# Modulation rows copied into weight order, one normalizing operation in place, and an earlier first gather

## The chip, the core and the metric

The kernel runs on one core of a Trainium2 chip. Its time is the device time of one execution, in microseconds (us). A core has five engines that run their own instruction queues in order: TensorE (PE, matrix products; its weight loads are listed as PEld), VectorE (DVE), ScalarE (ACT), GpSimd (POOL) and SyncE (SP, which only issues DMAs). POOL and ACT issue DMAs too.

## The reference, cut to what matters

Two layers work on 256 latent tokens and 256 context tokens of width 1024. Each layer has a mixer (attention, with an output projection) and then a mixture of 16 experts, two of which are chosen per token. Between them stands the part that the change touches:

```
x = x + g1 * y                                   # y: the mixer after its output projection
h = rms_norm(x) * (1 + sc2) + sh2                # rows sc2, sh2 differ for latent and context tokens
x = x + g2 * hierarchical_moe(h, ...)            # top-1 group, top-2 experts of 16
```

Layer 0 does this for latent and context tokens (four blocks of 128 tokens), layer 1 for the latent ones only (two blocks).

## The kernel before, in words

**Tiles.** `xt` holds the token blocks (tb) as 128 tokens by 1024 columns. `out_project` (L482) multiplies the mixer's result with the output weights in two halves of 512 columns (h) and, in each half, block by block (n). Every product is three matmuls of rounded parts (`mm3`, L315); the parts are made by `split` (L311), a cast on ACT and a subtraction on DVE. At the end of a block DVE scales the product by the row g1 (L497) and adds it to `xt` (L499), and `x_ready` (L1082) is called; `hook` (L1125) is called after each of the eight steps kt and places small work between the matmuls: folding the modulation into the router weights (`fold_mod`), transposes of `xt` (`x_turned`), router logits (`logits`).

**Normalization.** `x_ready` sums squares on ACT (L1086). After the second half it makes 1/rms (L1088, L411, L412) and the normalized block `h2[tb]` in two operations: L1092 multiplies `xt` by 1/rms and by the scale row, L1094 adds the shift row. The expert weights are stored with columns in another order ("weight order": column q*8+k goes to place k*128+q), so `h2` is written in that order, and L1092 and L1094 read `xt` and the rows with a step of 8 numbers (`by_part`, L1021). L1094 runs on DVE, but for the last block on POOL:

```
V.scalar_tensor_tensor(xp, by_part(xt[:, tb, :], KT), ss[:, tb, 4:5], scale, op0=ALU.mult,
                       op1=ALU.mult)
(G if tb == tbs[-1] else V).tensor_tensor(out=xp, in0=xp, in1=shift, op=ALU.add)
```

In layer 0 POOL then writes `h2` to DRAM (L1096). The rows are broadcast to all partitions by DMAs that POOL issues (`mod_row`, L372). One tile `rows` with one buffer holds both rows of a token kind, so that the context rows are fetched when the latent rows have been read. In layer 0 `h2` has a tile of its own; in layer 1 it stands in `xt[:, 2:4]`, which attention has used before.

**Experts.** After the last logits come some matmuls that only keep PE busy (`warm`, L226) and the routing on DVE (L1168 to L1453). The experts' work is cut into blocks of 128 slots, each with a gate (G), an up (U) and a down (D) product. Block 0 takes its tokens from `h2` by one-hot matmuls (`pick`, L1274). In layer 0 the later blocks fetch theirs from DRAM: `fetch_rows` (L1226) makes eight one-hot matrices on DVE (L1357), multiplies them on PE (L1233), sums to an index (L1237), and POOL issues a gather (L1239); `x_turn` (L1396) transposes the rows (L1409). `fetch_to` (L1414) is called in `gate_up` (L1623) after a gate product and asks for the rows of up to five blocks ahead. Expert weights are loaded by SP in pieces of 2 MB (L211) into a ring of buffers, each load waiting for a buffer to come free; most depend on the routing, which names the expert.

**Order.** A planner places the instructions of each engine by priority (the order of the program text) and by its own estimates of when they are ready; each engine then runs its list in order.

Of the kernel before, what the change touches and what calls it, by code (L numbers as in the profile page):

```python
# [11 lines left out]
F32 = mybir.dt.float32  # L12
# [4 lines left out]
ALU = mybir.AluOpType  # L17
AX = mybir.AxisListType

P = 128  # L20
D = 1024
KT = 8
# [143 lines left out]
def hybrid_kernel(ctx: ExitStack, tc: tile.TileContext, A: dict, dbg=None):  # L166
    nc = tc.nc
    V, S, T, G = nc.vector, nc.scalar, nc.tensor, nc.gpsimd
# [25 lines left out]
    def right(name):  # L194
        return Open(name, "right")
# [21 lines left out]
    def mm(name="mm"):  # L217
        return psum.tile([P, 512], F32, name=name, tag="mm", bufs=5)
# [15 lines left out]
    xt = pool.tile([P, 4, D], F32, name="xt")  # L234
# [42 lines left out]
    def load_router(wk, l):  # L277
        w = wk.tile([P, KT, 32], F32, name="wrt")
        V.memset(w, 0.0)
        G.dma_start(w[:, :, 0:4], A["w_group"][l].rearrange("(k p) g -> p k g", p=P))  # L280
        G.dma_start(w[:, :, 4:20], A["w_router"][l].rearrange("(k p) g -> p k g", p=P))
        return w
# [16 lines left out]
    h2d = dram.tile([512, D], F32, name="h2d")  # L299
# [72 lines left out]
    def mod_row(dst, l, seg, v, queue=G):  # L372

        queue.dma_start(dst, modd[l][seg, v:v + 1, :].to_broadcast([P, D]))
# [35 lines left out]
    def rstd_of(dst, ss, n, tmp):  # L410
        S.activation(tmp, ss, AF.Sqrt, bias=eps, scale=1.0 / n)  # L411
        V.reciprocal(dst, tmp)  # L412
# [608 lines left out]
    def by_part(a, k):  # L1021

        return a.rearrange("p (q k) -> p k q", k=k)

    def parted(a, k):

        return a.rearrange("p (k q) -> p k q", k=k)
# [5 lines left out]
    def moe(l, ntb, experts, yp, yT, finish, w_o, place, after_loads):  # L1033
        NT = 128 * ntb
        nv = (ntb + 1) // 2
        caps = CAPS[l]
        tbs = tuple(range(ntb))
# [7 lines left out]
        h2 = [xt[:, 2 + tb, :] if l else rows_of[:, tb, :] for tb in tbs]  # L1045
# [4 lines left out]
            experts.issue(1)  # L1050
        wk = right("out")
        wrt = load_router(wk, l)
        g1, rows = [], []
        for v in range(nv):
            g1.append(wk.tile([P, D], F32, name="g1", bufs=nv))
            mod_row(g1[v], l, 2, v)
        for v in range(nv):
            rows.append(wk.tile([P, 2, D], F32, name="rows", bufs=1))
            mod_row(rows[v][:, 0, :], l, 4, v)
            mod_row(rows[v][:, 1, :], l, 3, v)  # L1060

        wm = [wk.tile([P, KT, 32], F32, name="wm", bufs=1) for v in range(nv - 1)] + [wrt]
        crow = [wk.tile([P, 20], F32, name="crow", bufs=nv) for v in range(nv)]
# [1 line left out]
        def fold_mod(v):  # L1065
            sh, sc = (modr[l][:, i, :, v:v + 1].to_broadcast([P, KT, 32]) for i in range(2))
            t = wk.tile([P, KT, 32], F32, name="wsh", tag="rs", bufs=2)
            V.tensor_tensor(out=t, in0=wrt, in1=sh, op=ALU.mult)
            part = wk.tile([P, 32], F32, name="part", bufs=nv)
            V.reduce_sum(part, t.rearrange("p k e -> p e k"), axis=AX.X)  # L1070
            V.tensor_tensor(out=wm[v], in0=wrt, in1=sc, op=ALU.mult)
            if v == 0:
                V.memset(full, 1.0)
            ps = mm("crow")
            T.matmul(ps[:, 0:32], full, part, start=True, stop=True)
            V.tensor_tensor(out=crow[v], in0=ps[:, 0:20], in1=bias[:, 20 * l:20 * l + 20], op=ALU.add)

        full = wk.tile([P, P], F32, name="full", tag="lT", bufs=1)
        ss = wk.tile([P, ntb, 5], F32, name="ss")
        xT, pr, written = {}, [], []  # L1080

        def x_ready(h, tb):  # L1082

            c = slice(512 * h, 512 * h + 512)
            sq = wk.tile([P, 512], F32, name="sq", tag="rs", bufs=2)
            S.activation(sq, xt[:, tb, c], AF.Square, accum_out=ss[:, tb, h:h + 1])  # L1086
            if h:
                V.tensor_tensor(out=ss[:, tb, 2:3], in0=ss[:, tb, 0:1], in1=ss[:, tb, 1:2], op=ALU.add)  # L1088
                rstd_of(ss[:, tb, 4:5], ss[:, tb, 2:3], D, ss[:, tb, 3:4])
                xn = h2[tb]  # L1090
                xp, scale, shift = parted(xn, KT), *(by_part(rows[tb // 2][:, i, :], KT) for i in range(2))
                V.scalar_tensor_tensor(xp, by_part(xt[:, tb, :], KT), ss[:, tb, 4:5], scale, op0=ALU.mult,  # L1092
                                       op1=ALU.mult)
                (G if tb == tbs[-1] else V).tensor_tensor(out=xp, in0=xp, in1=shift, op=ALU.add)  # L1094
                if l == 0:
                    written.append(G.dma_start(h2d[128 * tb:128 * tb + 128, :], xn))  # L1096

        def x_turned(h, tb):
            pt = tr()
            for j in range(4):  # L1100
                kt = 4 * h + j
                T.transpose(pt[:, 128 * j:128 * j + 128], xt[:, tb, 128 * kt:128 * kt + 128], ident)
            xT[h, tb] = wk.tile([P, 4, P], F32, name=f"xT{h}", bufs=2 - h)
            (S.copy if h else V.tensor_copy)(xT[h, tb], pt.rearrange("p (k t) -> p k t", k=4))
# [20 lines left out]
        def hook(h, n, kt):  # L1125
            if h == 0 and n == 0 and finish:
                next(steps, None)
            if h == 0 and n == 1 and kt in (3, 6) and kt < 3 * nv + 3:
                fold_mod(kt // 3 - 1)
            if h == 1 and kt == 2:  # L1130
                x_turned(0, tbs[n])
            if h == 1 and n and kt == 4:
                x_turned(1, tbs[n - 1])
            if h == 1 and n >= 1 and kt >= KT - 2:
                if kt == KT - 2:
                    lgs[n - 1] = logits(tbs[n - 1])
                next(lgs[n - 1])
# [88 lines left out]
        def fetch_rows(i, hot):  # L1226
# [9 lines left out]
            with nc.allow_low_precision("whole numbers below 512"):  # L1236
# [5 lines left out]
        fixed_of = [[(r - experts.known, n_) for _, n_, r in b] for b in blocks  # L1242
                    if min(r for _, _, r in b) >= experts.known]
# [79 lines left out]
        for nm in ("base", "cap"):  # L1323
            t = un.tile([P] + sq, F32, name="cmp_" + nm, tag="aT", bufs=AB)
# [27 lines left out]
        def fetch(i):  # L1352

            def hot(o, tb, k):
                c = 0
                for s0, n_ in runs(i):
                    V.tensor_scalar(o[:, c:c + n_], C("iota128")[:, 0:n_], float(s0), slot[k][:, tb:tb + 1],  # L1357
                                    op0=ALU.add, op1=ALU.is_equal)
                    c += n_

            fetch_rows(i, hot)
# [52 lines left out]
        def fetch_to(i):  # L1414
            while l == 0 and fetched[0] < min(i, len(blocks)):
                fetch(fetched[0])
                fetched[0] += 1
# [212 lines left out]
        def down(bi, amid, final):  # L1630
# [29 lines left out]
            else:  # L1660
# [8 lines left out]
                if bi == len(blocks) - 2:  # L1669
                    for _ in range(3):  # L1670
                        experts.issue(1, queue=S)

        for i, (which, bi) in enumerate(ops):
            now[0] = i
            before = ops[i - 1] if i else None
            then = ops[i + 1] if i + 1 < len(ops) else None
            final = l == 0 and bi == len(blocks) - 1

            def amid(k):
                if k == 1 and then and then[0] == 0:  # L1680
                    x_turn(then[1])
                if k == 3 and final and which == 0:
                    weigh_last()
                if k == 2 and before and before[0] == 1:
                    for q in range(2):
                        a_turn(before[1], q)

            if final and which == 0:
                inorder = tc.manual_schedule(engines={mybir.EngineType.DVE, mybir.EngineType.Activation,
                                                      mybir.EngineType.PE})  # L1690
                inorder.__enter__()
            if which < 2:
                gate_up(which, bi, amid)
            else:
                down(bi, amid if before != (1, bi) else lambda k: amid(k) if k != 2 else None, final)
            if final and which == 0:
                for tb, tag, bufs in ((2, "xg", 2), (3, "xTb", XB)):
                    done = gather(tb, [un.tile([P, D], F32, name="yg", tag=tag, bufs=bufs) for k in range(2)])
                    pass
                after_loads(gather(0, [g2[:, nv + k, :] for k in range(2)]))  # L1700
            if final and which == 2:
                inorder.__exit__(None, None, None)
            if l and i == 0:
                ready(0, hot_rows(0))
# [4 lines left out]
        with tc.If(rv > 0):  # L1709
# [17 lines left out]
            with tc.For_i(0, NE, 1) as e:  # L1727
# [3 lines left out]
                with tc.If(nc.values_load(some[0:1, 0:1], min_val=0, max_val=1) > 0):  # L1731
# [7 lines left out]
                    for tb in range(ntb):  # L1739
# [4 lines left out]
                        for half in range(2):  # L1744
                            pt = tr()
                            for j in range(4):
                                kt = 4 * half + j
# [21 lines left out]
                        for h in range(2):  # L1769
                            ps = tr("dn")  # L1770
                            for f in range(4):
                                T.matmul(ps, aT[:, f, :], ws[2][:, f, 512 * h:512 * h + 512], start=(f == 0), stop=(f == 3))
                            t = un.tile([P, DE], F32, name="sg", bufs=SG)
                            V.scalar_tensor_tensor(t, ps, rc[:, tb:tb + 1], g2[:, tb // 2, 512 * h:512 * h + 512],
                                                   op0=ALU.mult, op1=ALU.mult)
# [7 lines left out]
        if l:  # L1783
            for tb, h in itertools.product(tbs, range(2)):
                c = slice(512 * h, 512 * h + 512)
                xn = un.tile([P, 512], F32, name="xn", tag="aT" if h else "sg", bufs=2)
# [75 lines left out]

    w_o, w_out = w_out, []
    rest, close_moe, gathers, tail = moe(0, 4, ex, yp, yT, None, w_o, place, after0)

    loads1 = [lambda: load_out("w_out_odd")]
# [51 lines left out]
```

## Time and profile before

| | us |
|---|---|
| median of 3 runs | 1079.56 |
| lowest, highest | 1076.38, 1085.37 |
| profiled execution | 1080.66 |
| its span in the trace | 1078.9 |
| PE busy in the span | 986.9 |
| DVE, ACT, POOL busy | 562.4, 385.0, 54.3 |

The span runs from the first to the last instruction in the trace; 1.8 us of the profiled execution lie around it. Busy times are sums; whether an engine holds up the others is read from the idle time in front of the waiting instructions.

### The profile page before, as it was taken

How to read it: one execution, taken by the hardware profiler on the slowest of the kernel's cores; microseconds unless marked ns; L12 is line 12 of the kernel's file. 1: busy time of each engine (PE TensorE's matmuls, PEld its weight loads, DVE VectorE, ACT ScalarE, POOL GpSimd, SP SyncE). 2: the span in 40 equal slices, each digit the busy share in tenths (PEclk: the TensorE clock that was granted, in tenths of full speed). 3: DMA queues.
4: the chain of work that ended last, by engine and by line, in shares of the span. 5: the costliest groups of instructions: out<-in, count | busy, mean ns of one | idle time of the engine just before them, and what ended most of it. 6: DMA issues, size and time to landing. Idle time of an engine off the chain costs nothing. (4 is left out here: it accounts for less than half of the span.)

```text
span 1078.9 us, 14186 instructions
## 1 busy us (share of the span) xinstructions
PE 986.9 (91%) x5205; PEld 579.3 (54%) x5205; DVE 562.4 (52%) x1346; ACT 385.0 (36%) x811; POOL 54.3 (5%) x75
## 2 busy tenths in 40 slices
PE   4899999896979989999987999998897999999995
PEld 3666555684543636567422668885566444434532
DVE  3565465767553636369316745627878323214324
ACT  4254343432132515368214525326853310100111
POOL 3000100102000000000021000000011000000000
PEclk8899999997989989999999999999997999999998
DMA  9969877525777999888896684234064899969891
GB/s 287 364 244 388 335 316 278 197 92 191 278 318 286 389 425 429 341 345 344 337 366 233 250 334 140 98 145 164 20 228 174 364 426 427 426 285 418 359 404 40
DMA packets 52546, 309.81 MB, mean 287 GB/s; under 512 B 4432, under 2 KB 12832, under 8 KB 35064
## 3 DMA queue, kind: packets, MB, share of 16 engines
q1 hardware_dynamic: 42440, 277.01, 64.9%
q0 software_dynamic: 5984, 19.26, 5.0%
q10 hardware_dynamic: 4048, 12.59, 3.1%
q8 instruction: 43, 0.70, 0.3%
q14 instruction: 31, 0.25, 0.1%
HBM read 299.85 MB, written 8.98 MB: 286 GB/s over the span
## 5 line engine op out<-in xcount | busy, mean ns | idle before, releaser
L1649 PE MATMUL dn<-we,aT 128*64 128x512 f32 (+2 forms) x480 | 119.4, 605 | 2.8 <-DMA we<-in_w_down_dram 2.7
L1616 PE MATMUL gu<-we,xT 128*64 128x512 f32 (+1 forms) x512 | 113.7, 611 | 1.7 <-DMA we<-in_w_up_dram 1.7
L1616 PE MATMUL gu<-we,xt 128*32 128x512 f32 (+2 forms) x448 | 104.9, 596 | 0.0
L312 ACT CAST wh<-we 128x512 fp32r<-128x512 f32 x144 | 85.4, 620 | 51.9 <-PE dn L317 28.5
L316 PE MATMUL mm<-wh,hT 128*128 128x512 f32 x248 | 101.5, 409 | 1.8 <-ACT hT L312 1.8
L313 DVE TENSOR_TENSOR wl<-we,wh 128x512 fp32r<-128x512 f32 x144 | 92.8, 685 | 17.2 <-ACT wh L312 11.3
L317 PE MATMUL mm<-wh,hT 128*128 128x512 f32 x248 | 98.5, 397 | 0.4 <-DVE hT L313 0.4
L318 PE MATMUL mm<-wl,hT 128*128 128x512 f32 x248 | 98.4, 397 | 0.0
L1649 PEld LDWEIGHTS dn<-we,aT 128*64 128x64 f32 (+2 forms) x480 | 36.4, 134 | 68.0 <-issue 62.1
L1616 PEld LDWEIGHTS gu<-we,xt 128*32 128x32 f32 (+2 forms) x448 | 36.5, 136 | 58.1 <-issue 56.2
L1616 PEld LDWEIGHTS gu<-we,xT 128*64 128x64 f32 (+1 forms) x512 | 32.9, 133 | 59.9 <-issue 56.6
L313 DVE TENSOR_TENSOR wl<-wi,wh 128x512 fp32r<-128x512 f32 x52 | 35.6, 688 | 50.1 <-ACT wh L312 35.0
L1627 DVE TENSOR_TENSOR sg<-sg,gu 128x256 f32<-128x256 f32 x40 | 15.2, 416 | 85.2 <-PE gu L1616 83.4
L316 PEld LDWEIGHTS mm<-wh,hT 128*128 128x128 f32 x248 | 47.3, 191 | 19.1 <-issue 7.3
L312 ACT CAST wh<-wi 128x512 fp32r<-128x512 f32 x52 | 32.1, 621 | 67.1 <-PE mm L317 62.8
L317 PEld LDWEIGHTS mm<-wh,hT 128*128 128x128 f32 x248 | 47.2, 190 | 11.5 <-issue 1.7
L318 PEld LDWEIGHTS mm<-wl,hT 128*128 128x128 f32 x248 | 47.1, 190 | 11.4 <-issue 0.8
L1622 ACT ACTIVATE sg<-gu 128x512 f32<-128x512 f32 x20 | 11.9, 596 | 90.6 <-PE gu L1616 84.5
L312 ACT CAST y<-y 128x512 fp32r<-128x512 f32 x16 | 9.9, 618 | 94.1 <-DVE y L1547 81.2
L345 PE MATMUL ada<-wada,cs 128*32 128x512 f32 x320 | 41.2, 619 | 2.4 <-DMA wada<-in_w_ada_dram 2.4
L316 PE MATMUL mm<-wo,yT 128*128 128x512 f32 x96 | 39.6, 413 | 2.4 <-ACT wo L312 2.4
L1357 DVE TENSOR_SCALAR oh<-cst,slots 128x128 bf16<-128x128 f32 (+1 forms) x96 | 23.4, 280 | 34.4 <-PE tok L1233 33.5
(364 smaller groups left out, 1675.3 us busy)
## 6 DMA issues: line engine op xcount, KB each, us to landing
we<-in_w_gate_dram SPq DMA_DIRECT2D x32, 2048.0 KB, 22.8
we<-in_w_up_dram SPq DMA_DIRECT2D x31, 2048.0 KB, 17.8
we<-in_w_down_dram SPq DMA_DIRECT2D x30, 2048.0 KB, 19.3
wada<-in_w_ada_dram SPq DMA_DIRECT2D x24, 2048.0 KB, 12.0
wi<-in_w_in_odd_dram SPq DMA_DIRECT2D x6, 2048.0 KB, 7.9
win<-in_w_in_even_dram SPq DMA_DIRECT2D x2, 2048.0 KB
wo<-in_w_out_even_dram SPq DMA_DIRECT2D x2, 2048.0 KB, 8.4
we<-in_w_down_dram ACTq DMA_DIRECT2D x2, 2048.0 KB, 13.8
```

The source lines that it names most:

```text
L312: S.copy(hi, src)
L313: V.tensor_tensor(out=lo, in0=src, in1=hi.bitcast(F32), op=ALU.subtract)
L316: T.matmul(ps, a[0], b[0], start=start, stop=False)
L317: T.matmul(ps, a[1], b[0], start=False, stop=False)
L318: T.matmul(ps, a[0], b[1], start=False, stop=stop)
L345: T.matmul(ps[32 * j:32 * j + 32], cs[:, kt, :], w[:, k, 512 * j:512 * j + 512], start=(kt == 0), stop=(kt == KT - 1))
L1357: V.tensor_scalar(o[:, c:c + n_], C("iota128")[:, 0:n_], float(s0), slot[k][:, tb:tb + 1], op0=ALU.add, op1=ALU.is_equal)
L1616: T.matmul(ps[c:c + n_], xTs[bi][0][:, kt, c:c + n_], experts.w[r, which][:, kt, :], start=(kt == 0), stop=(kt == KT - 1))
L1622: S.activation(parted(sgs[bi], 4), by_part(ps, 4), AF.Silu)
L1627: V.tensor_tensor(out=sg[:, c], in0=sg[:, c], in1=up[:, c], op=ALU.mult)
L1649: T.matmul(ps[h][c:c + n_], aTs[bi][0][:, f, c:c + n_], experts.w[r, 2][:, f, 512 * h:512 * h + 512], start=(f == 0), stop=(f == 3))
```

## The change

The scale and shift rows are fetched by DMA into tiles of `h2` that are not in use yet, and ACT copies them into weight order into tiles of their own (`take_row`): two scale tiles in layer 0 and one in layer 1, and one shift tile. `x_ready` no longer multiplies by the scale row with 1/rms. Instead `scaled` multiplies `xt` by the scale row, one half of the columns at a time: the first half at step 3 of the block, the second one in `x_ready`. One operation then multiplies by 1/rms and adds the shift row, in place and without steps in its reading, on DVE for all blocks. In layer 0 the row fetches for the context tokens stand at the end of the first half's second block. Last, the rows of the second expert block are asked for before the loop over the products.

```diff
-        for v in range(nv):
-            rows.append(wk.tile([P, 2, D], F32, name="rows", bufs=1))
-            mod_row(rows[v][:, 0, :], l, 4, v)
-            mod_row(rows[v][:, 1, :], l, 3, v)
+        arrived = {}
+        def fetch_row(i, v):
+            t = h2[0 if l else 2 + i]
+            mod_row(t, l, 4 - i, v)
+            arrived[i, v] = t
+        def take_row(i, v):
+            t = wk.tile([P, D], F32, name="shift" if i else "scale", bufs=1 if i else nv)
+            S.copy(parted(t, KT), by_part(arrived.pop((i, v)), KT))
+            row_of[i, v] = t
+        row_of = {}
+        fetch_row(0, 0)
+        if l == 0:
+            fetch_row(1, 0)
...
+        def scaled(h, tb):
+            part = lambda a: parted(a, KT)[:, :, 64 * h:64 * h + 64]
+            V.tensor_tensor(out=part(h2[tb]), in0=by_part(xt[:, tb, 512 * h:512 * h + 512], KT),
+                            in1=part(row_of[0, tb // 2]), op=ALU.mult)
         def x_ready(h, tb):
...
             if h:
+                scaled(1, tb)
                 V.tensor_tensor(out=ss[:, tb, 2:3], in0=ss[:, tb, 0:1], in1=ss[:, tb, 1:2], op=ALU.add)
                 rstd_of(ss[:, tb, 4:5], ss[:, tb, 2:3], D, ss[:, tb, 3:4])
-                xn = h2[tb]
-                xp, scale, shift = parted(xn, KT), *(by_part(rows[tb // 2][:, i, :], KT) for i in range(2))
-                V.scalar_tensor_tensor(xp, by_part(xt[:, tb, :], KT), ss[:, tb, 4:5], scale, op0=ALU.mult,
-                                       op1=ALU.mult)
-                (G if tb == tbs[-1] else V).tensor_tensor(out=xp, in0=xp, in1=shift, op=ALU.add)
+                V.scalar_tensor_tensor(h2[tb], h2[tb], ss[:, tb, 4:5], row_of[1, tb // 2], op0=ALU.mult, op1=ALU.add)
                 if l == 0:
-                    written.append(G.dma_start(h2d[128 * tb:128 * tb + 128, :], xn))
+                    written.append(G.dma_start(h2d[128 * tb:128 * tb + 128, :], h2[tb]))
+                    if tb == 1:
+                        take_row(1, 1)
...
+            if h == 0 and n == 1 and kt == 1:
+                take_row(0, 0)
+                if l:
+                    fetch_row(1, 0)
+            if h == 0 and n == 1 and kt == KT - 1:
+                take_row(1, 0)
+                if l == 0:
+                    fetch_row(0, 1)
+                    fetch_row(1, 1)
+            if h == 0 and n == 3 and kt == 2:
+                take_row(0, 1)
+            if h == 1 and kt == 3:
+                scaled(0, tbs[n])
...
+        fetch_to(len(fixed_of) + 1)
         for i, (which, bi) in enumerate(ops):
```

## Rows read from the trace of the kernel before

**Rows 1.** The page's first part: busy time of each engine.

```profile
PE 986.9 (91%) x5205; PEld 579.3 (54%) x5205; DVE 562.4 (52%) x1346; ACT 385.0 (36%) x811; POOL 54.3 (5%) x75
```

**Rows 2.** Windows: length, PE, PEld, DVE, ACT, POOL busy; PE clock; DMA share; GB/s.

```profile
245.00:260.00 15.00, 10.27 (x82) 7.89 (x83) 10.85 (x14) 2.93 (x9) 2.12 (x4) 0.90 0.61 218
260.00:275.00 15.00, 10.05 (x63) 7.83 (x56) 13.57 (x48) 2.68 (x6) 3.44 (x2) 0.53 0.65 238
...
290.00:305.00 15.00, 8.52 (x46) 3.75 (x45) 5.12 (x20) 0.86 (x2) 1.98 (x2) 0.77 0.99 423
...
320.00:335.00 15.00, 15.00 (x75) 6.57 (x73) 5.39 (x16) 3.15 (x7) 0.94 (x1) 1.00 0.25 68
```

**Rows 3.** Timeline, layer 0's last blocks: start, length, engine, line, [idle before <-releaser].

```profile
253.10 2.13 DVE L1092 SCALAR_TENSOR_TENSOR h<-xt,ss,rows 128x1024 f32<-128x1024 f32 x1 [2.00 <-DMA rows<-modd]
...
255.26 2.00 DVE L1094 TENSOR_TENSOR h<-h,rows 128x1024 f32<-128x1024 f32 x1
257.17 0.69 DVE L497 TENSOR_TENSOR rs<-mm,g 128x512 f32<-128x512 f32 x1
...
258.75 1.09 PE L1102 MATMUL tr<-cst,xt 128*128 128x128 f32 x4 [4.74 <-DVE xt L499]
...
260.94 2.10 DVE L1092 SCALAR_TENSOR_TENSOR h<-xt,ss,rows 128x1024 f32<-128x1024 f32 x1
...
261.67 0.63 PE L1118 MATMUL lg<-fold,lT 128*128 128x32 f32 x2 [0.44 <-ACT lT L1113]
...
262.96 0.23 DVE L1119 SCALAR_TENSOR_TENSOR lg<-lg,ss,crow 128x20 f32<-128x20 f32 x1
...
263.55 2.87 POOL L1094 TENSOR_TENSOR h<-h,rows 128x1024 f32<-128x1024 f32 x1 [5.45 <-DVE gm L1168]
263.62 2.83 DVE L1169 TENSOR_TENSOR gd<-lg,gm 128x16 f32<-128x16 f32 x1
```

**Rows 4.** Windows of half a microsecond, PE alone: length, PE busy; clock; DMA; GB/s.

```profile
254.00:254.50 0.50, 0.02 (x1) 1.00 0.96 393
...
308.50:309.00 0.50, 0.50 (x4) 1.00 0.92 393
```

**Rows 5.** Timeline, layer 0: the first gather, from its one-hots to its reader.

```profile
277.29 0.47 DVE L1357 TENSOR_SCALAR oh<-cst,slots 128x128 bf16<-128x128 f32 x2
...
286.71 0.20 PE L1233 MATMUL tok<-tokid,oh 128*128 128x2 bf16 x2
...
291.54 1.02 POOL L1239 DMA_INDIRECT xg<-h2d,ix  x1 [24.25 <-DVE wl L313]
...
302.53 1.09 PE L1409 MATMUL tr<-cst,xg 128*128 128x128 f32 x4 [6.48 <-DMA xg<-h2d,ix]
```

**Rows 6.** Lines of the combination in layer 0: operations on 1024 columns without steps.

```profile
L1502 DVE SCALAR_TENSOR_TENSOR yg<-yg,early x2: 1279/1282/1285, 566.7 to 578.7; 128x1024 f32<-128x1024 f32 x2
...
L1501 ACT ACTIVATE yg<-yg,early x2: 1148/1150/1152, 560.4 to 577.4; 128x1024 f32<-128x1024 f32 x2
```

**Rows 7.** Timeline, layer 1: casts of output weights, the last block, the routing.

```profile
797.57 2.72 ACT L312 CAST wo<-wo 128x512 fp32r<-128x512 f32 x4 [0.95 <-DVE lo L313]
...
807.79 0.69 DVE L497 TENSOR_TENSOR rs<-mm,g 128x512 f32<-128x512 f32 x1 [1.92 <-PE mm L318]
...
815.45 0.68 DVE L497 TENSOR_TENSOR rs<-mm,g 128x512 f32<-128x512 f32 x1
...
821.54 2.85 POOL L1094 TENSOR_TENSOR xt<-xt,rows 128x1024 f32<-128x1024 f32 x1 [32.64 <-DVE lg L1119]
...
821.70 2.73 DVE L1181 TENSOR_TENSOR ed<-lg,em 128x32 f32<-128x32 f32 x1
```

**Rows 8.** Windows of one microsecond in layer 1, PE alone.

```profile
815.00:816.00 1.00, 0.10 (x1) 1.00 0.48 98
...
829.00:830.00 1.00, 1.00 (x7) 0.50 0.00 0
```

**Rows 9.** DMAs that fill the tile rows: from issue to landing.

```profile
DMA to landing us min/median/max: 4.6/5.7/10.0
```

More of the change, by code (lines that the diff above doesn't have):

```diff
@@ L1052, in moe @@
         wrt = load_router(wk, l)
-        g1, rows = [], []
+        g1 = []
         for v in range(nv):
```

## The prediction

> **What bounds the kernel now.** I read the page's engine totals first: PE is busy for 91% of the span [rows 1], so only what makes PE stand counts, and a shorter DVE or POOL operation is worth something only where PE waits for it. The windows of 15 us show where PE stands around the change: of 15 us it misses 4.7, 5.0 and 6.5 in the windows from 245, 260 and 290 us, and none in the one from 320 [rows 2]. The timeline gives the three causes in layer 0.
>
> First, the end of the output projection. L1092 of the third block starts 2.00 us late, because the context rows come late, and with L1094 it holds DVE from 253.1 to 257.2. The g1 product of the last block (L497), ready when PE ends at 254.0, starts at 257.17, and PE's transposes wait 4.74 us [rows 3, 4]. Second, the routing. L1169, an operation on 16 numbers, takes 2.83 us, exactly beside POOL's L1094 of 2.87 us; L1119 before it waits for the end of L1092 [rows 3]. Third, the first gather is issued at 291.54 and PE stands 6.48 us for its rows [rows 5].
>
> Layer 1 has the second cause in full (L1181 takes 2.73 us beside POOL's 2.85) and a little of the first [rows 7, 8].
>
> **Late context rows and two long operations, layer 0.** L1092 and L1094 take about 2.1 us each on reads with steps; the same kind of operation on 1024 columns without steps takes 1.28 us [rows 3, 6]. So the new in-place operation costs 1.28, and each new half (512 columns, `xt` still read with steps) about half of 2.1, an estimate of 1.1 us. In place of 4.2 us behind 1/rms there are 1.3; the first half lies earlier in the block, the second beside ACT's sum of squares, where DVE waits anyway. DVE's load of a block falls by 0.7 us, so nothing piles up. The context rows are fetched in the first half of the columns already, so the 2.00 us go. The third block's operation, from about 251.5 (253.10 less the 2.00, and 0.4 for the second half ahead of it), ends before 253, the first half of the last block by about 254.1, and L497 starts then: **3.0 us** off 257.17. POOL's queue only gains: its write of the second block's `h2` stood behind the context row fetches and no longer does.
>
> **The last block.** The matmul that feeds L1119 ends at 262.30; with 1.28 in place of 2.10 us in front, L1119 starts at about 262.35 in place of 262.96: **0.6 us**. The second half puts 1/rms off by some 0.3 us, which ACT's transposed copy hides: the root waits behind it already. POOL's add is gone and so is the blocked 2.6 us of L1169: **2.6 us**. What is late next is the rest of the DVE routing chain, unchanged.
>
> **The first gather.** Eight one-hots, eight small matmuls, one sum and the DMA move ahead of block 0's 32 gate matmuls. Now the matmuls start at 286.71, after the gate, though the first one-hots are there at 277.3 [rows 5]. Asked for before the loop they fall into the gate at the latest, 7 us sooner; the gather then is issued 7 us sooner too, lands by 295.5 at the 11 us that it took, and PE needs it at 296.05 (302.53 less 6.48): **6.5 us**. The gather also goes ahead of the next weight loads on the DMA engines, which are short of work there. PE's stand also brought its clock to half; the full clock is back by 308.5 [rows 4], so some 5.8 us of work ran at half clock. Bounds 0 and 2.9 us; I take **1.5**, since the split rows of block 1 come through ACT and DVE, which the clock does not help. The pick matmuls before the gate ran partly at half clock too, 0.53 on the mean of 260 to 275 [rows 2]: between 0 and, for half of some 3 us, 1.6; the routing in front still leaves PE standing, so I take 0.
>
> **Layer 1.** L497 of the last block starts at 815.45, PE is done at about 815.0 [rows 7, 8]: 0.4. L1119 as above: 0.6. The blocked L1181: 2.5. Together **3.5 us**. The pick matmuls behind ran at half clock from 828.5 to 833.9 (one row of it: [rows 8]); with the wait in front shorter, PE's filler matmuls may keep the clock up. Bounds 2.5 gained and 1.0 lost (the fillers now end after the routing's first result and make it wait); I take **1.0** gained.
>
> **What is added.** Six ACT copies with steps, four in layer 0 and two in layer 1. No row shows such a copy; ACT without steps takes 1.15 us, DVE's operation with these steps 2.2 [rows 3, 6]. I take 2.0, nearer to the row with the same steps. The Trainium skill (SBUF — State Buffer, § Door 1: The DMA port swizzle) speaks against the copies: memory lines are 16 bytes, and a read that goes to a new line each time pays a penalty. DVE's rows agree (2.1 with steps, 1.28 without); no row shows it for ACT. By it the copies would cost about 2.2 us each, 13 us of ACT in all; at ACT's row without steps it would be 7 us.
>
> Each copy can also wait for its row, 4.6 to 10.0 us after the issue [rows 9]. In layer 0 the first two stand where ACT has nothing but sums of squares that nobody hurries for, the last between squares and transposed copies; the third stands at the start of the second half's weight casts, and its row has been asked for some 6 us before. In layer 1 two copies share one staging tile, so the second row is fetched only after the first copy, at about 800.5, and lands at 805 to 811. Behind it on ACT may stand casts of output weights, which run from 797.57 on [rows 7] and feed PE. DVE too: the first `scaled` of layer 1 writes the staging tile and must wait for the second copy, and L497 of 807.79 stands behind it. Bounds: 0, where the planner puts casts first, and 5 us per place, where PE runs out of cast weights; I take **1.0 us** lost in all.
>
> **Whether it stays.** Everything behind moves with PE: weight loads wait for buffers that PE frees, and in 320 to 335 us the DMA share is 0.25 with PE full [rows 2], so the loads carry no backlog across. I count no loss later.
>
> **Sum.** 3.0 + 0.6 + 2.6 + 6.5 + 1.5 + 3.5 + 1.0 - 1.0 = 17.7 us. Against the profiled execution, 1080.66: **1063 us**. That execution is 1.1 us above the median of the runs shown.
>
> **Rivals.**
> *A. The gather stays late.* The planner keeps the small matmuls behind the gate, or DVE makes the one-hots later. For it: they depend on the end of the routing. Against: with the one-hots at 277 there were 9 us in which only the order held them back. Gain 17.7 - 8.0 = 9.7: 1071 us. Chance 0.12.
> *B. The row copies hold ACT in both layers.* One place in layer 0 (context scale) and one in layer 1 (shift) make PE wait about 5 us each in place of 1 in all: 18.7 less 10 is a gain of 8.7, with one place 13.7: 1067 to 1072. Chance 0.15.
> *C. Slower: the wait for the rows replaces the wait for DVE.* The copies stand ahead of the second half's casts on ACT's in-order queue, and each waits its row's full 10.0 us [rows 9] plus 2.0 of copy; three such places (context scale in layer 0, both copies in layer 1) are 36 us, less some 6 us of casts in hand: 30 of standing, less the 18.7 that the other terms give, is 11 us slower, 1092. It decides from about 6 us of PE standing at each place. For it: no row shows where the planner puts the copies. Against: the median landing is 5.7 [rows 9], and the first row of either layer has some 10 us to come. Chance 0.05.
> *D. The start is gained and given back.* The weight loads saturate the DMA engines later (share near 1 in 290 to 305 [rows 2] already), and the experts' stage ends when they do: gain 3 to 6, 1076. Against: the 0.25 above. Chance 0.06.
>
> **How the numbers follow.** The forecast has the remaining 0.62; its own range is 1056 (all three clock bounds and nothing lost, 23.2 us, and the 1.1 us to the median) to 1069. With A and the lower part of B the range goes to 1074; C, D and the rest of B, under 0.2, are left out. Runs spread by 0.8%, so about 1%, 10.8 us, is what can be told from no change: faster needs less than 1068.8. That is most of the forecast and a part of B: 0.68. Within 1%: A, most of B, D, 0.26. Slower: C and a little, 0.06.
>
> **What would show it.** Right: no DVE operation of 2 us or more in the routing; L497 of layer 0's last block within 0.3 us of PE's end; no wait of PE for the rows of block 1; in-place operation near 1.3, halves near 1.1, ACT copies near 2.0 us. Wrong: PE waiting for `wo` casts with ACT idle for a DMA in front, the small matmuls still behind the gate, or PE waits for weights that were not there before.

## The result and the profile after

The changed kernel takes **1066.45 us** (median of 4 runs, 1060.02 to 1066.68) against 1080.26 for the kernel before in the same comparison: a ratio of **0.9855, 95% interval [0.9808, 0.9902]**: some 15.7 us by that ratio, 13.8 between the medians. Two repeats gave 1066.14 us, ratio 0.9856 [0.9836, 0.9876], and 1064.55 us, ratio 0.9862 [0.9834, 0.9890]. So there are three profiled executions of it, of 1060.02, 1066.14 and 1064.62 us; I call them the first, second and third. The forecast was 1063.

The page of the first, its first part, answers to [rows 1]:

```profile
PE 977.3 (92%) x5205; PEld 573.3 (54%) x5205; DVE 556.4 (53%) x1354; ACT 397.3 (38%) x817; POOL 48.9 (5%) x73
```

ACT has 12 us more, DVE 6 and POOL 5 less. The time is PE's idle time and its clock, so I cut the executions at eleven instructions that each of them has and compare the stretches from start to start (worked out from the timelines; "gain" is before less after).

| stretch, us | before | first | second | third | forecast gain | gains |
|---|---|---|---|---|---|---|
| up to layer 0's first cast of output weights | 202.28 | 198.67 | 200.57 | 199.81 | 0 | 3.6, 1.7, 2.5 |
| to its first g1 product (L497) | 6.90 | 6.89 | 6.90 | 8.40 | 0 | 0.0, 0.0, -1.5 |
| to the last block's g1 product | 47.99 | 45.12 | 45.11 | 45.09 | 3.0 | 2.9, 2.9, 2.9 |
| to the first pick matmul | 13.61 | 9.68 | 9.68 | 9.70 | 3.2 | 3.9, 3.9, 3.9 |
| to the first gate matmul | 8.91 | 8.80 | 8.99 | 9.97 | 0 | 0.1, -0.1, -1.1 |
| to the fourth gather | 46.67 | 39.06 | 39.06 | 39.05 | 8.0 | 7.6, 7.6, 7.6 |
| to layer 1's attention (L906) | 403.97 | 404.19 | 408.44 | 405.88 | 0 | -0.2, -4.5, -1.9 |
| to layer 1's first cast of output weights | 55.14 | 53.63 | 53.61 | 55.16 | 0 | 1.5, 1.5, 0.0 |
| to the last block's g1 product | 29.98 | 33.83 | 33.73 | 32.65 | -0.6 | **-3.9, -3.8, -2.7** |
| to the first pick matmul | 13.05 | 11.19 | 11.13 | 9.21 | 3.1 | 1.9, 1.9, 3.8 |
| to the first gate matmul | 6.32 | 3.90 | 3.91 | 3.91 | 1.0 | 2.4, 2.4, 2.4 |

The first row lies ahead of what the change touches, and its gain is not the change's: over the fourteen executions that this document uses it runs from 198.2 to 202.9 us, with the kernel before near the upper end. The stretches that the forecast names (those with a forecast gain or loss, and layer 0's pick matmuls, put at 0) gave 15.0, 14.9 and 17.0 us. Layer 0's three gains that were forecast are the same to a few hundredths in all executions; layer 1's projection lost where next to nothing was expected.

Windows of the first execution, columns as in [rows 2]: layer 0's last blocks, its routing and pick matmuls, its gate; then two short ones in layer 1, for below.

```profile
242.00:257.00 15.00, 12.29 (x85) 8.85 (x85) 11.41 (x29) 6.04 (x14) 1.07 (x2) 1.00 0.52 200
257.00:272.00 15.00, 12.15 (x94) 9.99 (x94) 11.14 (x58) 1.38 (x3) 0.00 (x0) 0.89 0.83 317
271.00:286.00 15.00, 15.00 (x73) 5.09 (x73) 7.18 (x24) 4.62 (x7) 1.99 (x2) 1.00 0.70 262
...
787.00:790.00 3.00, 3.00 (x10) 2.36 (x10) 3.00 (x6) 0.72 (x2) 0.00 (x0) 0.66 0.00 0
...
811.00:815.00 4.00, 3.94 (x36) 3.76 (x38) 3.96 (x17) 0.59 (x1) 0.00 (x0) 1.00 0.00 0
```

In the first three PE misses 2.7 and 2.9 us where it missed 4.7 and 5.0, and none in the gate with the gather behind it.

Timelines of the first execution in layer 0: DVE's last block (against [rows 3]), PE beside it, then the first gather (against [rows 5]).

```profile
250.68 0.69 DVE L497 TENSOR_TENSOR rs<-mm,g 128x512 f32<-128x512 f32 x1 [2.18 <-PE mm L318]
...
253.99 1.28 DVE L1111 SCALAR_TENSOR_TENSOR h<-h,ss,shift 128x1024 f32<-128x1024 f32 x1
255.19 0.23 DVE L1138 SCALAR_TENSOR_TENSOR lg<-lg,ss,crow 128x20 f32<-128x20 f32 x1
255.86 0.17 DVE L1201 TENSOR_TENSOR gd<-lg,gm 128x16 f32<-128x16 f32 x1
...
252.26 0.63 PE L1121 MATMUL tr<-cst,xt 128*128 128x128 f32 x4 [1.48 <-DVE xt L499]
...
269.04 0.19 PE L1265 MATMUL tok<-tokid,oh 128*128 128x2 bf16 x2
...
273.30 1.02 POOL L1271 DMA_INDIRECT xg<-h2d,ix  x1 [17.20 <-DVE oh L1389]
...
281.30 0.55 PE L1441 MATMUL tr<-cst,xg 128*128 128x128 f32 x3
```

L497 now waits for PE, not PE for it: the transposes wait 1.48 us in place of 4.74. The 16-number operation takes 0.17 us in place of 2.83. The small matmuls start inside the gate, the gather goes out at 273.30, and its reader L1441 shows no wait.

Layer 1's projection in the first execution: ACT, then DVE, then PE.

```profile
779.55 2.33 ACT L1068 COPY shift<-xt 128x1024 f32<-128x1024 f32 x1
781.75 1.17 ACT L312 CAST wo<-wo 128x512 fp32r<-128x512 f32 x2
...
782.43 0.69 DVE L313 TENSOR_TENSOR lo<-wo 128x512 fp32r<-128x512 f32 x1 [1.49 <-ACT wo L312]
783.04 0.42 DVE L1082 TENSOR_TENSOR wsh<-wrt,modr 128x256 f32<-128x256 f32 x1
784.37 0.59 DVE L1084 TENSOR_REDUCE part<-wsh 128x32 f32<-128x256 f32 x1
...
785.01 0.41 PE L1089 MATMUL crow<-part,full 128*128 128x32 f32 x2 [2.02 <-DVE part L1084]
```

ACT's shift copy stands in front of a weight cast, DVE's subtraction waits 1.49 us for that cast, `fold_mod` stands behind the subtraction on DVE, and PE waits 2.02 us for its sum. In the window behind, from 787 us, PE is busy throughout but its granted clock is 0.66. The second and third executions show the same wait with 1.92 and 2.24 us. In the second the clock falls to 0.50 as well (window from 793.3 to 795.3 us). In the third it stays at 1.00 behind the wait (794 to 798 us), and its stretch lost 1.1 to 1.2 us less than the other two.

Layer 1's routing in the first execution (against [rows 7, 8]):

```profile
799.87 0.69 DVE L497 TENSOR_TENSOR rs<-mm,g 128x512 f32<-128x512 f32 x1 [2.52 <-PE mm L318]
...
805.07 0.19 DVE L1213 TENSOR_TENSOR ed<-lg,em 128x32 f32<-128x32 f32 x1
807.54 0.19 DVE L1229 TENSOR_TENSOR Mb<-M,M 128x32 bf16<-128x32 f32 x1
...
804.35 5.38 PE L231 MATMUL warm<-cst 128*128 128x256 f32 x12
809.57 0.20 PE L1238 MATMUL pos<-Mb,ones 128*128 128x16 bf16 x2
811.06 3.98 PE L1316 MATMUL pick<-first,xt 128*128 128x128 f32 x32 [1.22 <-DVE first L1280]
```

The operation of 2.73 us takes 0.19. The routing's first result (`Mb`) is there at 807.73, but the position matmuls start at 809.57, behind the fillers; the pick matmuls then run at full clock (the window from 811 us), in 3.98 us. Before, they took 6.39:

```profile
828.50 6.39 PE L1284 MATMUL pick<-first,xt 128*128 128x128 f32 x32 [1.24 <-DVE first L1248]
```

### The profile page after: what moved, and what is told of

The parts are those of the page before. It is cut to its first block, busy times and chain, and to the rows that moved or that the text cites. A ratio compares the mean times of both kernels' runs of the same rounds, so it can differ in the third digit from the quotient of the medians.

```text
span 1058.3 us, 14182 instructions
## 1 busy us (share of the span) xinstructions
PE 977.3 (92%) x5205; PEld 573.3 (54%) x5205; DVE 556.4 (53%) x1354; ACT 397.3 (38%) x817; POOL 48.9 (5%) x73
## 5 line engine op out<-in xcount | busy, mean ns | idle before, releaser
L1648 PE MATMUL gu<-we,xT 128*64 128x512 f32 (+1 forms) x512 | 116.7, 616 | 4.3 <-DMA we<-in_w_up_dram 4.3
L312 ACT CAST wh<-we 128x512 fp32r<-128x512 f32 x144 | 85.4, 621 | 53.6 <-PE dn L317 27.4
```

Source lines behind the costliest of these rows:

```text
L312: S.copy(hi, src)
L1648: T.matmul(ps[c:c + n_], xTs[bi][0][:, kt, c:c + n_], experts.w[r, which][:, kt, :], start=(kt == 0), stop=(kt == KT - 1))
```

## The experiments

My theory was the forecast's, with two things added from the traces: layer 1's shift copy delays PE through `fold_mod`, and the experts' stage of layer 0 may give time back at its last weights. The rivals stand in each expectation. There are twelve experiments, in three groups, each with its own runs of the kernel before; the ratios are to those.

**The changed kernel again** (no edit), as the base for the others.

> The changed kernel itself, unaltered, as the base for the others and to see whether the profiled 1060.0 us or the 1066.5 us of its other runs is the usual one. The forecast's theory: 1063 to 1067 us, 13 to 17 us under the kernel before; in the profile the same terms (last block's g1 product right behind PE, no wait for the first gather, some 2 us of PE waiting for layer 1's folded router part behind the shift copy). Rival (the profiled run was only a lucky one and one of the terms is not there in others): over 1068 us, with a PE wait for gathered rows or a routing operation of over 2 us in its trace.

1066.14 us; the 1060.02 of the first profile was a lucky one. The second profile differs from the first by 1.9 us in front of the change and by 4.3 us between the fourth gather and layer 1; the terms are the same.

**The gather's call taken out of the changed kernel.**

```diff
-        fetch_to(len(fixed_of) + 1)
```

> The changed kernel without the one line that asks for the first gather ahead of the loop. Theory (the first gather's early call is worth 6.5 us of standing and 1.5 us of clock): 7 to 9 us slower than the changed kernel, with a PE wait of 5 to 7 us for the gathered rows of block 1 back in the trace. Rival (the wait is only moved, and is given back where the expert weights arrive last): within 2 us of the changed kernel, and PE waits longer for the last up and down weights in the changed one by as much as the gather's wait is shorter.

1072.79 us, ratio 0.9914 [0.9891, 0.9937]: 6.7 us slower than the changed kernel, just under the 7 to 9 and far from the rival's 2. The stretch from gate to fourth gather is 46.88 us, 7.8 longer, and PE's wait is back:

```profile
295.50 1.08 PE L1441 MATMUL tr<-cst,xg 128*128 128x128 f32 x4 [6.16 <-DMA xg<-h2d,ix]
```

**The gather's call alone, in the kernel before** (the same line added).

> The kernel before with that one line alone added: rows and the final add stay as they were. Theory: 7 to 9 us faster than before (about 1072 us), no PE wait for gathered rows of block 1, the routing operations of 2.8 us still there. Rival (the early call only pays because the routing ends sooner too): under 3 us.

1075.24 us, ratio 0.9938 [0.9915, 0.9960], 4 to 9 us faster, 5.7 between the medians where 7 to 9 was expected. The stretch is 39.04 us, 7.6 shorter, as with the whole change, and the blocked operation is still there (2.82 us). So the gather's worth doesn't hang on the rest; in the time it is some 6 to 7, a little less than in its stretch.

```profile
284.54 1.02 POOL L1239 DMA_INDIRECT xg<-h2d,ix  x1 [17.58 <-DVE oh L1357]
...
291.99 0.55 PE L1409 MATMUL tr<-cst,xg 128*128 128x128 f32 x3
```

**The last block's shift add on DVE, in the kernel before.**

```diff
-                (G if tb == tbs[-1] else V).tensor_tensor(out=xp, in0=xp, in1=shift, op=ALU.add)
+                V.tensor_tensor(out=xp, in0=xp, in1=shift, op=ALU.add)
```

> The kernel before with the last block's shift add put on DVE in place of POOL, in both layers. Theory (the 16-number routing operation takes 2.6 us too long because POOL's add shares its port): L1169 and L1181 fall from 2.8 to about 0.2 us, and an add of about 2.1 us stands on DVE ahead of the logits in each layer in its place, which delays them by up to 2.1 us: 0 to 3 us faster in all. Rival (the routing operation is slow by itself, or for its place): it stays at 2.7 us or more with POOL idle, and the time grows by 2 to 4 us.

1077.60 us, ratio 0.9943 [0.9919, 0.9967]: faster by more than expected. With POOL idle the routing operations take 0.17 us in layer 0 and 0.19 in layer 1; the add that stands in front costs 2.02 and 2.00. Layer 0's:

```profile
263.59 2.02 DVE L1094 TENSOR_TENSOR h<-h,rows 128x1024 f32<-128x1024 f32 x1
265.91 0.17 DVE L1169 TENSOR_TENSOR gd<-lg,gm 128x16 f32<-128x16 f32 x1
```

So it was POOL's add that made the operations slow. From g1 product to pick matmul the layers gain 0.8 and 1.2 us; 2.4 more come from layer 1's pick matmuls, which run at full clock here (3.90 us to the gate in place of 6.32). That the clock would follow is what my estimate lacked.

**Plain rows, in the kernel before.** Block and rows without steps, all else as before. This leaves out the weight order, so the experts compute other values, and only layer 0 up to its first gate matmul is compared.

```diff
-                xp, scale, shift = parted(xn, KT), *(by_part(rows[tb // 2][:, i, :], KT) for i in range(2))
-                V.scalar_tensor_tensor(xp, by_part(xt[:, tb, :], KT), ss[:, tb, 4:5], scale, op0=ALU.mult,
+                xp, scale, shift = xn, rows[tb // 2][:, 0, :], rows[tb // 2][:, 1, :]
+                V.scalar_tensor_tensor(xp, xt[:, tb, :], ss[:, tb, 4:5], scale, op0=ALU.mult,
```

> The kernel before, with the rows and the block read and written in their own order, without steps (the values then stand in another order, so what the experts compute, and layer 1's routing, are other ones: only layer 0 up to its first gate matmuls is compared closely). The rows still come late, the add stays on POOL and the gather stays late. Theory (3.0 us of layer 0 are 2.0 of late rows and the rest two long DVE operations, and the steps cost 0.8 us an operation): both DVE operations take 1.28 in place of 2.1 us, the wait for the rows stays at about 2.0, the last block's g1 product comes 1.3 to 1.7 us sooner relative to the first one, the logits' scaling behind the last block's operation 0.6 to 0.8 us sooner, and the routing operation of 2.8 us stays. Rival (the steps cost nothing, the operations are long for their operands): 2.1 us as before, nothing gained.

The time is 1071.61 us, ratio 0.9932 [0.9909, 0.9955], but it is not the price of the steps, as the work behind is another one. In layer 0 the stretch between first and last g1 product is 44.73 us, 3.3 shorter, where 1.3 to 1.7 was expected. The third block and the routing:

```profile
248.12 1.28 DVE L1092 SCALAR_TENSOR_TENSOR h<-xt,ss,rows 128x1024 f32<-128x1024 f32 x1
249.72 1.23 DVE L1094 TENSOR_TENSOR h<-h,rows 128x1024 f32<-128x1024 f32 x1 [0.31 <-DMA rows<-modd]
252.01 0.69 DVE L497 TENSOR_TENSOR rs<-mm,g 128x512 f32<-128x512 f32 x1 [1.07 <-PE mm L318]
...
257.24 2.30 DVE L1181 TENSOR_TENSOR ed<-lg,em 128x64 f32<-128x64 f32 x1
...
243.54 1.05 POOL L374 DMA_DIRECT2D rows<-modd  x2 [6.08 <-DVE h L1094]
...
257.12 2.34 POOL L1094 TENSOR_TENSOR h<-h,rows 128x1024 f32<-128x1024 f32 x1 [5.34 <-DVE lg L1119]
```

The steps cost 0.8 us an operation, as expected. But the wait for the context rows is gone as well, 0.31 us in place of 2.00: POOL can issue their fetch only when the second block's L1094 has read the old rows, so it is the long operations that made the rows late. The operation beside POOL's add is blocked here too (2.30 beside 2.34).

**Layer 1's shift copy later.** The row is staged in the other block's place, and the copy is put behind the second block's sum of squares on ACT.

```diff
-            t = h2[0 if l else 2 + i]
+            t = h2[i if l else 2 + i]
...
-            if h == 0 and n == 1 and kt == KT - 1:
-                take_row(1, 0)
+            if h == (1 if l else 0) and n == (0 if l else 1) and kt == (6 if l else KT - 1):
+                if l:
+                    with tc.issue_after(squares[-1].ins):
+                        take_row(1, 0)
```

> The changed kernel, with layer 1's shift row staged in the second block's place and its copy put on ScalarE behind the sum of squares of the second block, so that no weight cast of the projection stands behind it. Theory (this copy is what delays the casts, DVE's folded router part and the small matmul in front of which PE waits 1.9 to 2.0 us, and PE's clock falls behind that wait): the wait of the crow matmul falls under 0.5 us, the g1 product of the last block of layer 1 comes some 3 us sooner relative to the projection's first one; 2 to 4 us faster than the changed kernel, 1062 to 1064. Rival (the folded router part is late by itself, from the wait for PE and the scale copy): the wait stays at 1.5 us or more, and the time within 1 us.

1063.54 us, ratio 0.9838 [0.9807, 0.9868]; against the repeats of the changed kernel that is 1 to 2.6 us, which the intervals don't tell from nothing by themselves. The place does:

```profile
789.05 0.41 PE L1089 MATMUL crow<-part,full 128*128 128x32 f32 x2 [0.53 <-DVE part L1084]
...
792.13 2.31 ACT L1068 COPY shift<-xt 128x1024 f32<-128x1024 f32 x1
```

PE waits 0.53 us, a little over the 0.5 expected, and the stretch of the projection is 30.83 us in place of 32.65 to 33.83 (30.81 and 30.84 in the two later runs with this edit). The theory holds: this copy's place cost 1.8 to 3.0 us. The rest of the loss, 0.85 us more than in the kernel before, lies ahead of the first g1 product. The scale copy stands among the casts there, and DVE waits 0.88 us for the cast behind it; no run moved that copy.

**Three fillers in place of six in layer 1.**

```diff
-        warm(6 if l else 4, pr[-1])
+        warm(3 if l else 4, pr[-1])
```

> The changed kernel with 3 in place of 6 filler matmuls behind the logits of layer 1. Theory A (the fillers hold PE past the moment at which the routing's first result is there): the position matmuls of layer 1 start 1.5 to 2 us sooner and the time falls by 1 to 2 us. Theory B (the fillers carry PE to its full clock and the pick matmuls are what they pay for): the pick matmuls take 5 to 6.4 us in place of 4.0, and the time is the same or up to 1 us longer.

1065.61 us, ratio 0.9869 [0.9841, 0.9898]: no difference to the changed kernel. This experiment's timeline, then the third profile of the changed kernel:

```profile
803.58 1.54 PE L231 MATMUL warm<-cst 128*128 128x256 f32 x6
807.24 0.21 PE L1238 MATMUL pos<-Mb,ones 128*128 128x16 bf16 x2 [2.12 <-DVE Mb L1229]
808.74 5.46 PE L1316 MATMUL pick<-first,xt 128*128 128x128 f32 x32 [1.22 <-DVE first L1280]
```

```profile
809.76 2.84 PE L231 MATMUL warm<-cst 128*128 128x256 f32 x12
813.42 0.21 PE L1238 MATMUL pos<-Mb,ones 128*128 128x16 bf16 x2 [0.83 <-DVE Mb L1229]
814.92 3.98 PE L1316 MATMUL pick<-first,xt 128*128 128x128 f32 x32 [1.21 <-DVE first L1280]
```

Both theories were right, and cancel: counted from the last block's g1 product, the position matmuls come 1.9 to 2.0 us sooner than in the first two executions, and the pick matmuls take 1.5 longer. Against the third execution the position matmuls come no sooner. With six fillers it hangs on the clock at which they run: they take 2.84 us in the third profile and 5.38 in the first, and only the 5.38 us hold the routing up.

**Layer 0's last up weights ahead of the writes.** In the changed kernel DVE's copy of the last but one block's output waits for an earlier write of that tile, and the load of the last up weights stands behind the new writes on ACT's queue. The second profile:

```profile
516.54 0.33 SPq L211 DMA_DIRECT2D we<-in_w_up_dram  x1
...
519.50 0.90 ACTq L1699 DMA_DIRECT2D yd<-y  x2
...
530.24 0.69 DVE L1695 COPY y<-dn 128x512 f32<-128x512 f32 x1 [8.96 <-DMA yd<-y]
...
533.61 0.53 ACTq L211 DMA_DIRECT2D we<-in_w_up_dram  x1
...
542.03 9.24 PE L1648 MATMUL gu<-we,xT 128*64 128x512 f32 x30 [5.18 <-DMA we<-in_w_up_dram]
```

Before, SP's load went out 3 us behind that write, the copy waited for PE and not for the write, and PE waited 1.72 us for the up weights and 2.66 for the down weights:

```profile
533.95 1.75 ACTq L1667 DMA_DIRECT2D yd<-y  x2
...
537.13 0.33 SPq L211 DMA_DIRECT2D we<-in_w_up_dram  x1
...
543.24 0.69 DVE L1663 COPY y<-dn 128x512 f32<-128x512 f32 x1 [7.54 <-PE dn L1649]
...
555.00 7.08 PE L1616 MATMUL gu<-we,xT 128*64 128x512 f32 x30 [1.72 <-DMA we<-in_w_up_dram]
...
567.35 2.58 PE L1649 MATMUL dn<-we,aT 128*64 128x512 f32 x6 [2.66 <-DMA we<-in_w_down_dram]
```

Two things speak against a loss here. PE's two waits together were 4.4 us before and 4.3, 5.7 and 4.8 in the three executions of the changed kernel. And the delayed write is not the change's alone: in the kernel before with the add on DVE, SP's load went out 2.5 us ahead of the write too, and the copy waited 7.25 us. The edit issues the last up load first:

```diff
+                    if bi == len(blocks) - 2:
+                        experts.issue(1, queue=S)
+                        then_y.enter_context(tc.issue_after(more["sent"].ins))
                     V.tensor_copy(y[0], ps[0])
                     S.copy(y[1], ps[1])
...
-                    for _ in range(3):
+                    for _ in range(2):
                         experts.issue(1, queue=S)
```

> The changed kernel, with the last up weights of layer 0's experts asked for ahead of the last but one block's output copy and writes on ScalarE's queue, not behind them. Theory (the changed kernel gives 3 to 5 us back here: the output copy waits 9 us for an earlier write that now shares the DMA engines with a weight load, and the up load stands behind it, so PE waits 5.2 us in place of 1.7): the load goes out some 5 us sooner relative to the stage, PE's wait for up weights falls under 1 us; 3 to 5 us faster than the changed kernel, 1061 to 1063. Rival (the load is limited by the DMA engines, which are full there, or by its place coming free, and not by the queue): PE waits as long, for up or for down weights, and the time stays within 1 us.

1062.18 us, ratio 0.9836 [0.9806, 0.9867], in the expected range, though the intervals don't tell it from the repeats of the changed kernel. The load goes out 3.1 us behind the write's issue in place of 14.1. PE's wait for up weights is gone, but one for down weights takes its place, as the rival has it:

```profile
522.70 0.39 ACTq L211 DMA_DIRECT2D we<-in_w_up_dram  x1
...
550.00 9.25 PE L1681 MATMUL dn<-we,aT 128*64 128x512 f32 x30 [4.37 <-DMA we<-in_w_down_dram]
```

From DVE's output copy ahead of the delayed write to the last operation of the combination the changed kernel took 45.7, 46.5 and 46.2 us and this one 44.2; but the two experiments on layer 1, which lack this edit, took 44.8 and 44.4. So this run alone doesn't show where its gain comes from.

**The same edit in the kernel before.**

> The kernel before, with the last up weights of layer 0's experts asked for ahead of the last but one block's output copy and writes, as in the run with the up load first. Theory (the changed kernel gave back 3 us at this place because its earlier weight load delayed a write, so before there is less to win): 0 to 2 us faster than before, PE's wait for up weights from 1.7 to 0 and a longer one for down weights. Rival (the place was worth as much before the change, and nothing was given back there): 4 us or more faster.

1076.00 us, ratio 0.9964 [0.9941, 0.9988], 1.3 to 6.4 us faster; the stretch to layer 1's attention falls from 403.97 to 400.22 us. At the place itself PE's waits for weights are down to 0.7 us, from 4.4, and from the output copy to the end of the combination it takes 40.4 us in place of 46.8. That is the rival's way: the place was worth as much before the change, though the interval of the time alone doesn't exclude the theory's 2 us. So the gain of the experiment ahead of this one doesn't prove that the change gave time back here.

**Both edits in the changed kernel.**

> The changed kernel with both: layer 1's shift copy behind the sum of squares, and the last up load of layer 0 ahead of the writes. If both theories hold, the gains add, as they lie in different stages: 5 to 9 us faster than the changed kernel, 1057 to 1061. If only one holds, its gain alone; if the time in front is always given back at a later load, less than 2 us.

1059.70 us, ratio **0.9798 [0.9764, 0.9833]**; within the noise the gains add. PE's wait for down weights is 1.7 us here, and the place takes 41.1 us.

**Changed kernel and both edits side by side.**

> The changed kernel, unaltered, on the same chip as the next one: 1064 to 1068 us.

> The kernel with the later shift copy and the earlier up load again, beside the changed kernel: 5 to 7 us faster than it, 1058 to 1061 us. If the earlier difference came from the chip and not from the edits, under 2 us.

1064.55 us, ratio 0.9862 [0.9834, 0.9890], and 1057.74 us, ratio **0.9787 [0.9760, 0.9815]**. The second is 6.8 us faster than the change and some 23 faster than the kernel before, and the intervals don't touch. In its profile the wait for down weights is 5.0 us and the place takes 44.6: the two edits together are worth 5 to 7 us, but what the earlier load brings of it differs between executions of the same kernel.

## Why the prediction was right, point by point

- **Late rows and two long operations, layer 0: 3.0, measured 2.9.** The sizes hold: the in-place operation takes 1.28 us, the halves 1.11 to 1.17. The cause was told half right. I put 2.0 of the 3.0 down to rows that come late and credited the earlier fetch; with plain rows and the old fetch the rows came in time by themselves.
- **The last block and the routing, layer 0: 3.2, measured 3.9.** The blocked operation gave its 2.6 us. The logits' scaling gained 1.3 in place of 0.6: PE's work in front of it ran at a granted clock of 1.00 in place of 0.50, so that its transposes took 0.63 us in place of 1.09.
- **The first gather: 8.0, measured 7.6** in the stretch, and 6 to 7 in the time. Rival A is excluded: the small matmuls did fall into the gate.
- **Layer 1: 3.5 in all, measured 0.4, 0.6 and 3.6.** This is where the forecast was mis-sized. "I take 1.0 us lost in all" for the copies stands against 2.7 to 3.9 us lost in the projection (with 0.4 gained forecast there). I had named the place (shift copy, casts behind it) and looked for PE running out of cast weights. The way was another: cast, subtraction, `fold_mod` behind it in order, and PE at a small matmul in the middle of a product. Where the clock fell behind the wait, in two of three executions, it cost 1.1 to 1.2 us more. It is rival B in one of its two places, with 1.8 to 3.0 us in place of about 5; in layer 0 DVE waits 2.50 us for a shift copy, and the stretch lost nothing. In part it came back: the pick matmuls gained 2.4 by the clock, near my upper bound of 2.5 in place of the 1.0 taken. The lower bound happened as well, in two of three executions: fillers at half clock held the routing up, 1.9 gained in place of 3.1.
- **The copies' own cost: 2.0 taken, 2.14 to 2.33 measured.** An ACT operation on 1024 columns without steps takes 1.15 [rows 6]. The rule of the Trainium skill (SBUF — State Buffer, § Door 1: The DMA port swizzle) is that a read which goes to a new 16-byte line each time pays a penalty; the trace agrees for ACT. The forecast's 2.2 by this rule was an estimate from DVE's rows.
- **"I count no loss later": no loss at the place suspected, the rest open.** From the fourth gather to layer 1 the changed kernel took 0.2, 4.5 and 1.9 us longer. Its wait for the last up weights was 4.3, 5.2 and 4.8 us in place of 1.7, but with the wait for down weights the sums are 4.3, 5.7 and 4.8 in place of 4.4, and the place as a whole took 45.7 to 46.5 us in place of 46.8. Behind it, up to layer 1's attention, the profile of the kernel before has the shortest time of all fourteen executions, 150.3 us (the changed kernel 151.6 to 153.4, the others 150.7 to 154.0). Kernels that differ from the one before only in the gather, the add or the plain rows took 1.1 to 3.0 longer in the stretch. So rival D at its full size (12 to 15 us given back) is excluded, and a loss of 2 us is not settled.
- **Rival C** (three waits of 10 us behind the copies): none is there.

In sum: 17.7 forecast, 14.9 to 17.0 measured in those stretches. The step that was mis-sized is the loss behind layer 1's copies: 2.1 to 3.3 us more in its projection, and 1.2 less gained in its routing in two of three executions. Some 0.7 in layer 0's routing and 1.4 in layer 1's pick matmuls went the other way; that they make up for part of it is luck. By the time alone 1064.6 to 1066.5 us lies about as near to rival B's 1067 for one place as to 1063; it is the stretches that tell the two apart.

## What to carry to other kernels

When a helper copy goes on an in-order engine, follow what stands behind it through the other queues: here 2.3 us on ACT reached PE by way of a cast, a subtraction and a fold on DVE. When a tile arrives late, ask first what frees its place; the cure may be a shorter reader and not an earlier fetch. Cut several executions at common instructions before explaining a difference of one pair of profiles: the steady stretches agree to hundredths, and the others show the spread.

## What the runs showed that was not expected

- **The clock gives whole steps.** Equal work takes one of two lengths: layer 0's way from the first cast to the first g1 product 6.9 or 8.4 to 8.5 us (granted clock 1.00 or 0.80 over it), attention of layer 1 53.6 or 55.1 (1.00 or 0.97), the twelve filler records 2.84 us at a granted clock of 1.00 (third profile) or 5.38 at 0.51 (first), the levels of 2.4 and 1.2 GHz. The length of the wait in front did not decide it: behind 2.02 and 1.92 us at layer 1's small matmul the clock fell to 0.50, behind 2.24 us it stayed at 1.00.
- **An operation on 16 to 64 numbers lasts as long as POOL's neighbour**: 2.30 us beside an add of 2.34 without steps, 2.73 and 2.83 beside adds of 2.85 and 2.87 with steps, 0.17 to 0.23 with POOL idle.
- **A write of 256 KB behind a load of 2 MB**: in the stage's last part the four writes took 10.6 us (median) to land in the second profile, where SP's load went out 3 us before two of them, and 3.2 in the kernel before, where it went out 3 us behind. In the fourteen executions the load went out 2.5 to 6.2 us ahead eleven times, and DVE's copy then waited 7.0 to 9.2 us for the write; three times it went out 2.2 to 5.0 us behind, and the copy waited for PE.
